# A three-pass encoder layer: later weights copied to bf16 during the first pass, conv matrices built there, and the third pass laid over buffers that the mixer frees first

## The chip, the cores and the metric

The kernel runs on all 8 cores of one Trainium2 chip, as two dies of four cores (0 to 3 and 4 to 7). The metric is device microseconds (us) of the slowest core. All cores run the same program on different rows; nothing is exchanged.

A program on all cores has a second, slower state in some executions: the cores of one die, or of both, then show a lower granted clock and the time is some per cent longer (in the first comparison one run of each kernel, 3149 and 3136 us). All comparisons below are between fast runs, or between cores of a die that kept its clock.

## The reference, cut to what matters

```python
def encoder_layer(x, ...):
    x = x + 0.5 * swiglu_ffn(x, g_ff1, w_ff1_in, w_ff1_out)      # first pass,  "A"
    z = rms_norm(x, g_mix) @ w_in                                # mixer, "B":
    cv, cg, q, k, v = jnp.split(z, SPLITS, axis=-1)
    u = cv * jax.nn.sigmoid(cg)                                  #   gated unit ...
    c_out = conv_tail(...)        # causal depthwise conv of 31 taps, layer norm, silu
    a_out = banded_window_attention(...)                         #   and attention
    x = x + jnp.concatenate([c_out, a_out], axis=-1) @ w_out     #   output projection
    x = x + 0.5 * swiglu_ffn(x, g_ff2, w_ff2_in, w_ff2_out)      # third pass, "C"
    return x, ...

def swiglu_ffn(x, g, w_up, w_down):
    a, b = jnp.split(rms_norm(x, g) @ w_up, 2, axis=-1)
    return (jax.nn.silu(a) * b) @ w_down
```

The model width is 1024 and the inner width of the feed-forward part 2816, that is 22 column groups of 128. Each core has 4096 prompt rows, 128 halo rows and 64 sample rows. Inputs and weights are fp32; the kernel multiplies in bf16.

## The kernel before

The kernel goes through its rows three times. Each pass has its own weights in SBUF, and a pass fills nearly all of SBUF, so a later pass's weights can be loaded only when an earlier pass lets go of the bytes.

Operations are recorded in program order and then put in order by a small list scheduler of the kernel's own. On each engine it may take an operation from among the first `WINDOW` that are still to be done. The order is fixed at build time, and waits come from the data that operations share.

```python
WINDOW = {"sync": 24, "scalar": 24, "vector": 24, "gpsimd": 24, "tensor": 24}
# ... Prog.schedule():
        def pick(e):
            q, h = queue[e], head[e]
            # ...
            while h < len(q) and seen < WINDOW[e]:
                u = q[h]
                h += 1
                if done[u]:
                    continue
                seen += 1
                # ... the first that is ready, or the one ready soonest
```

The feed-forward pass (used as A and as C) keeps all its weights in two tiles. The weights are fp32 in DRAM, and the loads cast them to bf16. The Trainium skill, "DMA: Bandwidth & Descriptors", section "SWDGE vs HWDGE vs iDMA", says that a cast during a DMA has to be issued from GpSimd; these loads are all on that queue.

```python
class FF:
    def __init__(self, K, off, tag, wu, wd, ...):
        C = Carve(K.P, off, tag)                       # hands out SBUF bytes in order
        self.WU = C([128, NJ, 2048], BF16, "wu")       # NJ = 22 column groups
        self.WD = C([128, NJ, 1024], BF16, "wd")
        # ... H, XNT, XA, XR, XB, XO, SA, G1, G2, SM
        self.PU = [K.pb[0], K.pb[1], K.pb[2], K.pb[3]] # PSUM banks of the up products
        self.PD = [K.pb[4], K.pb[5]]                   # and of the down products

    def load_w(self, j):
        self.O.dma("gpsimd", self.tag + "wu%d" % (j % 8), self.WU[:, j, :], self.wu[j])

    def up(self, bi, bg):                              # one block of up to 3 (first: 4) row groups
        for j in range(NJ):
            # ... 2 x 8 matmuls of 384 columns into two banks, Silu on ACT, product on DVE
            bg(1)                                      # a piece of the next block's norm
    # down(): for each row group and each half, 22 matmuls of 512 columns
```

The mixer's conv is done by matmuls against banded matrices (`wdc` in DRAM, read back as `B_wr`). They are built on DVE at the very start, between the weight loads:

```python
def conv_weights(K, off):
    # ... WB: two buffers
    def step(g):
        w = WB[g % 2]
        O.tt(w[:, :, :], EY[...], CO[:, g, :]..., ALU.mult)
        O.dma("gpsimd", "wdc%d" % (g % 2), d.wdc[g], w..., wk=[("wdc", g)])

    def prologue():
        step = conv_weights(K, A.wd_off + 15 * 2048)
        for j in range(NJ):
            A.load_w(j)
        for g in range(16):
            step(g)
        for j in range(NJ):
            A.load_d(j)
```

In the mixer the tiles matter that live to its end: `B_wo` (output weights), `B_ma` and `B_mc` (attention and conv output, transposed), `B_mt` (conv output on its way back through DRAM, `zd`), `B_wr`, `B_y`, and the three residual buffers `B_x`. The third pass was laid from the same base upward over all of this:

```python
    M = Mixer(K, base)
    M.setup()
    M.run()
    Cc = FF(K, base, "C", d.wu2, d.wd2, d.gains[2], None, ...)
    Cc.run(loads(Cc))
```

## Time and profile before

| | before |
|---|---|
| time, three runs | 2821.67, 2824.42 and (slow) 3149.47 us |
| span in the profile, slowest core (1) | 2817.9 us |
| TensorE busy | 2492 us, 88% |
| first pass, from the first down product on | 921 us |
| from the last conv product to the first down product of C | 244 us |

A row group is 128 rows, and a "down product" is one with `A_wd` or `C_wd`. Nearly every instruction goes through one helper line (L343), so the trace is read by tile names.

First, the page of the kernel before. Its 40 slices stand for 70 us each, and a digit is the share in tenths: TensorE busy, TensorE clock granted, DMA busy.

```profile
PE   1699999999999998888688962469999999999998
...
PEclk9899999999999998899799986779999999999999
DMA  9931222112221163223244559862111221111110
```

Counted from 1, TensorE is full except at the very start, in the mixer (slices 16 to 24) and in a hole in slices 25 to 27 (the digits 2, 4, 6). There DMA is the busy part, and the clock falls to 0.6.

The table of stretches of the kernel before, core 1. After each stretch come its length and then the busy time of five engines with the number of their instructions, the granted clock, the DMA share, and GB/s.

```profile
core 1: us, PE busy (x) PEld busy (x) DVE busy (x) ACT busy (x) POOL busy (x), PEclk, DMA share, GB/s
178.00:1092.00 914.00, 913.37 (x5439) 512.49 (x5439) 352.08 (x1072) 229.56 (x400) 54.72 (x81) 1.00 0.24 70
1612.10:1667.40 55.30, 39.26 (x252) 25.17 (x249) 31.07 (x63) 26.66 (x44) 10.17 (x17) 0.88 0.68 210
1667.40:1828.10 160.70, 65.81 (x262) 26.95 (x261) 44.28 (x81) 16.20 (x21) 39.55 (x72) 0.71 0.82 193
1828.10:1911.00 82.90, 55.81 (x411) 39.24 (x410) 35.42 (x127) 25.25 (x45) 9.02 (x17) 0.81 0.60 133
1715.00:1760.00 45.00, 1.01 (x2) 0.21 (x2) 0.76 (x2) 0.00 (x0) 14.83 (x27) 0.50 1.02 192
1550.00:1600.00 50.00, 48.07 (x318) 24.75 (x316) 27.02 (x60) 23.28 (x42) 7.46 (x13) 1.00 0.54 165
```

- The first pass (178 to 1092) cannot be had cheaper by moving work: 913 of 914 us busy, and DMA is only a quarter used. There is room for other DMA here.

- The casting loads reach 192 GB/s with DMA share 1.02. In another stretch 165 GB/s take a share of 0.54, which would be about 305 GB/s at full share (an estimate from that line). So bytes that a cast moves take about 1.6 times the DMA time.
- From 1715 to 1760 TensorE did 1 us of work, and its clock stands at 0.50. The Trainium skill, "TensorE: Matmul & The Clock Gate", Part 1, says that an idle window of about 3.4 us takes the clock to half. This trace agrees on the half; the 3.4 us it does not show. So idle time there costs twice: the work after it starts at half speed (four products of 1.86 us against 1.03, in the timeline below).

The chain of waits of the kernel before, core 1 (start, length, what was waited for or done):

```profile
35.53 24.49 DMA wdc<-W_wb
...
62.26 41.01 DMA wdc<-W_wb
...
173.07 5.70 DMA A_wd<-wd
...
1720.37 13.73 DMA C_wu<-wu
...
1736.39 25.41 DMA B_mt_161<-zd
...
1768.94 26.77 DMA x<-B_x_128
```

The conv matrices wait for their own stores (24 and 41 us), which stand in the GpSimd queue behind weight loads. The first down products then wait for their weights. Later, the weight loads of C make the conv output's way back (`B_mt`, 25 us) and a residual store (27 us) slow.

The timeline of TensorE in the kernel before (start, length, instruction, output<-inputs, count, and in brackets the idle time before it with what ended that):

```profile
62.10 20.52 PE L343 MATMUL PS<-A_xnt,A_wu 128*128 128x448 bf16 x96 [0.94 <-ACT A_xnt L343]
109.19 1.01 PE L343 MATMUL PS<-K_t,A_xb 128*128 128x128 bf16 x8 [26.58 <-DVE A_sm L343]
...
178.91 17.09 PE L343 MATMUL PS<-A_wd,A_h 128*128 128x512 bf16 x70 [0.63 <-DMA A_wd<-wd]
...
1740.54 1.01 PE L343 MATMUL PS<-B_wo,B_mc_145 128*128 128x512 bf16 x2 [30.14 <-DVE B_mc_145 L343]
1762.46 1.01 PE L343 MATMUL PS<-B_wo,B_mc_145 128*128 128x512 bf16 x2 [20.91 <-DVE B_mc_145 L343]
...
1804.11 1.86 PE L343 MATMUL PS<-B_wo,B_mc_145 128*128 128x512 bf16 x4 [26.16 <-DVE B_x_128 L343]
```

The hole at 82.6 in the first up run is 26.6 us. In the hand-over to C there are waits of 30.1, 20.9 and 26.2 us. Four products with `B_wo` take 1.86 us after a wait of 26 us; in an unbroken run they take 1.03.

How four late reads into `B_mt` (the four into its second buffer, tile `B_mt_161`) fared while C's weights were loaded, kernel before:

```profile
DMA to landing us min/median/max: 14.0/19.9/26.0
```

### The profile page before, as it was taken

To read this page: it belongs to the slowest core of one execution; us is meant where nothing else is said; L and a number is where in the kernel's file an instruction comes from. 1 tells how busy PE (TensorE), PEld (TensorE's weight loads), DVE (VectorE), ACT (ScalarE), POOL (GpSimd) and SP (SyncE) were. 2 spreads that over 40 slices of the span, in tenths; PEclk is the share of its full clock that TensorE was granted. 3 is DMA by queue.
4 is the path that set the end of the run, shared out by engine and by line. 5 is a ranking of instruction groups with operands and counts; after the bars stand their busy time and mean duration, and the time that the engine had idled before them with its cause. 6 is when DMAs were issued, how large, how long until landed. Compare 5 with 4: busy or idle time off the path is not lost.

```text
span 2817.9 us, 41303 instructions; the slowest of 8 cores (2803.6 to 2817.9 us)
## 1 busy us (share of the span) xinstructions
PE 2492.3 (88%) x14740; PEld 1365.4 (48%) x14740; DVE 1032.1 (37%) x2701; ACT 747.9 (27%) x1303; POOL 216.3 (8%) x380
## 2 busy tenths in 40 slices
PE   1699999999999998888688962469999999999998
PEld 0345555555555554334344530145555555555554
DVE  2243443334433333544647562143223332233211
ACT  1112222222222222545546440031112211122110
POOL 2110000000000011000111123110000000000000
PEclk9899999999999998899799986779999999999999
DMA  9931222112221163223244559862111221111110
GB/s 199 165 94 55 76 79 64 47 48 79 87 64 42 38 159 74 55 57 105 68 132 115 184 169 217 197 145 64 45 53 38 68 68 52 53 40 52 46 45 23
DMA packets 111521, 244.00 MB, mean 87 GB/s; under 512 B 32415, under 2 KB 49695, under 8 KB 111319
## 3 DMA queue, kind: packets, MB, share of 16 engines
q0 software_dynamic: 42592, 131.65, 18.4%
q1 hardware_dynamic: 68727, 109.70, 13.5%
q8 instruction: 121, 1.98, 0.3%
q14 instruction: 81, 0.66, 0.1%
HBM read 207.82 MB, written 74.79 MB: 100 GB/s over the span
## 4 chain that ended last, share of the span: by engine, by line
PE 81%; DMA 9%; DVE 4%; issue 3%; ACT 2%; POOL 0%; SPq 0%; DVEq 0%; POOLq 0%; ACTq 0%
PE PS L343 81%; DMA wdc<-W_wb 3%; DMA x<-B_x_128 1%; DMA W_ey<-eye 1%; DMA B_mt_161<-zd 1%; DMA B_mt_160<-zd 1%; DVE B_y L343 1%; DMA C_wu<-wu 0%; ACT B_pt L343 0%; DMA B_x_128<-x 0%; DMA C_xa<-x 0%; DVE W_wb L343 0%; DMA B_hc<-sconv 0%; DVE B_qn L343 0%; ACT B_sq L343 0%
## 5 line engine op out<-in xcount | busy, mean ns | idle before, releaser
L343 PE MATMUL PS<-A_xnt,A_wu 128*128 128x384 bf16 (+1 forms) x3872 | 652.8, 330 | 0.9 <-ACT A_xnt L343 0.9
L343 PE MATMUL PS<-C_xnt,C_wu 128*128 128x384 bf16 (+1 forms) x3872 | 628.5, 324 | 0.8 <-ACT C_xnt L343 0.8
L343 PEld LDWEIGHTS PS<-A_xnt,A_wu 128*128 128x128 bf16 x3872 | 378.0, 98 | 258.1 <-issue 6.4
L343 PEld LDWEIGHTS PS<-C_xnt,C_wu 128*128 128x128 bf16 x3872 | 378.2, 98 | 240.5 <-issue 1.4
L343 PE MATMUL PS<-A_wd,A_h 128*128 128x512 bf16 (+1 forms) x1496 | 329.3, 381 | 5.0 <-DMA A_wd<-wd 5.0
L343 PE MATMUL PS<-C_wd,C_h 128*128 128x512 bf16 (+1 forms) x1452 | 315.3, 379 | 0.0
L343 ACT ACTIVATE C_sa<-PS 128x384 f32<-128x384 f32 (+1 forms) x242 | 117.5, 485 | 706.3 <-PE PS L343 696.0
L343 DVE TENSOR_TENSOR C_h<-PS,C_sa 128x384 bf16<-128x384 f32 (+1 forms) x242 | 133.3, 551 | 345.9 <-PE PS L343 345.1
L343 DVE TENSOR_TENSOR A_h<-PS,A_sa 128x384 bf16<-128x384 f32 (+1 forms) x242 | 136.0, 563 | 308.4 <-PE PS L343 307.6
L343 ACT ACTIVATE A_sa<-PS 128x384 f32<-128x384 f32 (+1 forms) x242 | 119.7, 495 | 430.2 <-PE PS L343 379.9
L343 PEld LDWEIGHTS PS<-A_wd,A_h 128*128 128x128 bf16 (+1 forms) x1496 | 146.7, 98 | 179.4 <-issue 9.1
L343 PEld LDWEIGHTS PS<-C_wd,C_h 128*128 128x128 bf16 (+1 forms) x1452 | 142.4, 98 | 169.9 <-issue 0.4
L343 DVE SCALAR_TENSOR_TENSOR C_xr<-PS,C_xr 128x512 f32<-128x512 f32 (+1 forms) x66 | 45.6, 691 | 281.3 <-PE PS L343 281.3
L343 PE MATMUL PS<-B_xn,B_wi 128*128 128x512 bf16 x512 | 126.5, 398 | 8.5 <-DVE B_t_76 L343 3.4
L343 PE MATMUL PS<-K_t,A_xb 128*128 128x128 bf16 (+1 forms) x544 | 42.9, 224 | 84.1 <-DVE A_sm L343 62.6
L343 PE MATMUL PS<-B_us,B_wr 128*128 128x256 bf16 (+1 forms) x576 | 88.2, 309 | 30.2 <-DVE B_qkt L343 17.6
L343 DVE SCALAR_TENSOR_TENSOR A_xr<-PS,A_xr 128x512 f32<-128x512 f32 (+1 forms) x68 | 46.9, 690 | 163.3 <-PE PS L343 163.1
L343 PE MATMUL PS<-B_wi,B_xn 128*128 128x256 bf16 (+1 forms) x512 | 92.6, 335 | 8.3 <-ACT B_pt L343 8.3
L343 PE MATMUL PS<-B_wo,B_mc_145 128*128 128x512 bf16 x64 | 20.7, 453 | 83.0 <-DVE B_mc_145 L343 51.0
L343 ACT ACTIVATE A_xb<-A_xr 128x1024 bf16<-128x1024 f32 (+1 forms) x34 | 35.8, 1053 | 201.5 <-DVE A_xr L343 201.5
L387 POOL DMA_DIRECT2D yout<-C_xr x33 | 17.6, 535 | 928.2 <-DVE C_xr L343 928.2
L343 ACT ACTIVATE B_pt<-PS 128x1024 bf16<-128x1024 f32 (+1 forms) x68 | 66.1, 984 | 78.6 <-PE PS L343 78.6
(167 smaller groups left out, 2029.4 us busy)
## 6 DMA issues: line engine op xcount, KB each, us to landing
B_wr<-wdc SPq DMA_DIRECT2D x32, 576.0 KB, 5.0
A_xa<-xin SPq DMA_DIRECT2D x33, 512.0 KB, 3.9
A_xr<-xin SPq DMA_DIRECT2D x33, 512.0 KB, 3.6
x<-A_xr POOLq DMA_DIRECT2D x33, 512.0 KB, 3.0
C_xr<-x SPq DMA_DIRECT2D x32, 512.0 KB, 3.7
C_xa<-x SPq DMA_DIRECT2D x32, 512.0 KB, 3.7
yout<-C_xr POOLq DMA_DIRECT2D x32, 512.0 KB, 2.9
A_wu<-wu POOLq DMA_DIRECT2D x22, 512.0 KB, 37.1
```

The costliest lines, as they stand in the source:

```text
L343: o = self.P.add(eng, lambda e: getattr(e, meth)(**kw), r, w, cost=self.cost(eng, meth, kw))
L387: self.P.add(eng, lambda e: e.dma_start(out=out, in_=in_), r, w, lane=lane, rk=rk, wk=wk, cost=1.0 if eng == "gpsimd" else 0.5, nbytes=n * ...
```

## The change

The intent has three parts.

1. Start: no conv matrices between the first pass's weights. They are built in 32 halves during the first pass, in buffers of that pass (`XO`).
2. Copies: all later weights (`w_in`, `w_out`, and the third pass's two) are cast once, DRAM to DRAM, in 60 casting copies spread over the first pass. Later loads then are plain bf16 copies from the sync queue and carry half the bytes from DRAM.
3. Layout: C's tiles are put where the mixer frees its bytes first. The first 11 up weights lie over projection and attention tiles, the other 11 over the conv tiles. C has other PSUM banks for its up products. The scheduling window goes from 24 to 64, so that C's first norms and up products can be placed among the last output projections.

The diff, cut to its core:

```diff
-WINDOW = {"sync": 24, "scalar": 24, "vector": 24, "gpsimd": 24, "tensor": 24}
+WINDOW = {"sync": 64, "scalar": 64, "vector": 64, "gpsimd": 64, "tensor": 64}
...
+        fits = NJ if low is None else (low - c1.off) // 4096
+        self.WU = [(c1 if j < fits else c2)([128, 2048], BF16, "wu") for j in range(NJ)]
...
-        self.PU = [K.pb[0], K.pb[1], K.pb[2], K.pb[3]]
-        self.PD = [K.pb[4], K.pb[5]]
+        self.PU = [K.pb[2], K.pb[4], K.pb[3], K.pb[5]]
+        self.PD = [K.pb[0], K.pb[1]]
...
     def load_w(self, j):
-        self.O.dma("gpsimd", self.tag + "wu%d" % (j % 8), self.WU[:, j, :], self.wu[j])
+        k = [("pc", self.tag + "u", j)] if self.weng == "sync" else []
+        self.O.dma(self.weng, self.tag + "wu%d" % (j % 8), self.WU[j][:, :], self.wu[j], rk=k)
...
+    def hook(bi, j):
+        if bi == 0:
+            return
+        if j % 3 == 1 and casts:
+            t, k, dst, src = casts.pop(0)
+            O.dma("gpsimd", "pc%d" % (k % 4), dst, src, wk=[("pc", t, k)], after=P.last["vector"])
+        if j % 5 == 3 and convs:
+            wstep[0](*convs.pop(0))
...
     def prologue():
-        step = conv_weights(K, A.wd_off + 15 * 2048)
-        for j in range(NJ):
-            A.load_w(j)
-        for g in range(16):
-            step(g)
-        for j in range(NJ):
-            A.load_d(j)
+        loads(A)()
+        wstep[0] = conv_weights(K, cr, lambda: A.XO[A.nxt("xo", 2)])
...
-    Cc = FF(K, base, "C", d.wu2, d.wd2, d.gains[2], None, ...)
+    c0 = Carve(P, base, "C")
+    c2 = Carve(P, M.US_off, "C_")
+    Cc = FF(K, (c0, c0, c2), "C", d.wu2b, d.wd2b, d.gains[2], None, ..., low=M.mid, weng="sync")
```

## The prediction

> **What bounds the kernel now.** By the table of stretches: three PE-bound passes with two DMA holes. First pass, 178 to 1092 us: PE 913 of 914 us busy, clock 1.00, DMA share 0.24. Mixer, 1092 to 1710: PE 503 of 618, limited by short ACT/DVE/PE dependencies. Third pass, 1883 to 2817: PE 99% busy, clock 1.00. The holes:
> - Start (chain of waits, 0 to 179 us): the conv matrices' DVE products wait for their own stores (24.5 and 41.0 us), which queue behind weight casts; norms and gating sit behind them on DVE. PE idles 26.6 us at 82.6; down starts at 169, stalls, and runs freely from 178.9.
> - Mixer to third pass, 1710 to 1883: PE busy 63 of 173 us at clock 0.66, DMA share 0.88 at 188 GB/s. Casting weight loads start at 1715; the B_mt reads then take 20-25 us instead of 4, residual traffic waits likewise (chain: 25.4, 26.8, 13.7 us).
>
> **What DMA costs.** Casting loads move 196 GB/s (of destination) at share 1.0; elsewhere 165 GB/s take only 0.54, about 305 GB/s per full share. So 17.3 MB of third-pass weights cost about 88 us as casts, about 57 us as bf16 copies (estimates from those figures). The Trainium skill, "DMA: Bandwidth & Descriptors", section "Issuing engines are not separate DMA queues", says queues share the same 16 engines; the trace agrees: a sync-queue A_xa load took about 31 us under casts, median 3.9.
>
> **What the change does.**
> 1. Start: no conv matrices between weights. The third row block's x still lands near 50 us, so up products start near 60 as now, then run without the hole: 352 matmuls at about 0.19 us = 67-70 us; down starts near 132-135, weights landed (about 21 MB/196 = 107 us). Gain: about 40 us.
> 2. Sixty casts (23 MB, about 120 us of DMA) and 32 DVE products of about 0.7 us spread over the first pass: DMA share about 0.4, PE above 98%. Loss 0 to 10 us.
> 3. Mixer: work unchanged; the wider scheduling window leaves PE order nearly the same. Within 15 us either way.
> 4. Third pass: 11 of 22 up weights overlay attention buffers, so they load during the conv tail (DMA share 0.6 there; may cost the tail 10 us); first norms and half of the first up run among the last out-projections, on other PSUM banks. Only 11.5 MB remain. Of the 173-us hole about 52 us is PE work at full clock; I expect 10-25 us of stalls left (last up and down weights, after the last out-projection). Gain 90-105 us.
>
> Sum: 40 + 97 + 5 - 5 = about 140 us, nearly all on the critical path. Predicted 2680 us, range 2635 to 2730. Faster by over 2%: 0.95; within 2%: 0.04; slower: 0.01.
>
> **What would show it.** Step 1: first long down run starts at 130-140, PE dense from about 60. Step 2: PE 98% or more at clock 1.00 in the first pass. Step 4: weight issues from the sync queue start when attention ends; B_mt reads land in under 8 us; PE holes between mixer and third pass total under 40 us. Mixer length (first pass end to last conv matmul, now about 580 us) within 15 us.
>
> **What would make it wrong.** First-pass residual traffic caught behind casts, or ACT's copies waiting for the buffers that conv stores share, would stall PE there. Early weight loads on the in-order sync queue could hold up conv-matrix and history loads, lengthening the tail by tens of us. The order is static: a wait the scheduler misjudged now blocks more. Conversely, if the mixer packs better, the time falls below 2650.

## More of the kernel before

- Between the last conv product (1667) and the first down product of C (1911) TensorE is busy for 66 and then 56 us, 122 of 244. The other 122 us are idle.

## The result, and the profile after

| | before | after |
|---|---|---|
| median of four runs each | 2823.14 us | 2731.5 us |
| fast runs | 2821.67, 2821.85, 2824.42 | 2720.68, 2724.05, 2738.95 |
| slow run | 3149.47 | 3135.9 |
| ratio of fast runs, 95% | | 0.9664 [0.9608, 0.972] |
| span in the profile, slowest core | 2817.9 (core 1) | 2722.3 (core 3) |
| TensorE busy | 88% | 92% |

A ratio is the mean time of one kernel's fast runs over that of the other's of the same rounds, so it is not quite the ratio of the medians. The medians here also carry the one slow run of each kernel.

The change took about 95 us here, and 102 us in a later measurement (run after_again below, 0.9636). The prediction was a gain of about 140. The direction and most of the size came; some 40 us did not.

To see where, each profile was cut into stages by the starts of the first and last matmuls of a group. The figures are means over cores 0 to 3 in us, from starts read to whole us, so a stage is good to about half a us and a sum to about one:

| stage (from, to) | before | after | difference |
|---|---|---|---|
| start: 0 to the first down product of A | 166.8 | 125.3 | -41.5 |
| A: to the last down product of A | 920.8 | 927.8 | +7.0 |
| attention: to the last product of `B_pt` (p times v) | 519.0 | 522.3 | +3.3 |
| conv tail: to the last conv product | 55.0 | 69.3 | +14.3 |
| outputs: to the last output projection | 159.5 | 132.0 | -27.5 |
| C: to the last down product of C | 979.8 | 930.3 | -49.5 |
| sum | 2800.8 | 2706.8 | -94.0 |

The page of the kernel after, read as before:

```profile
PE   2999999999999998887779965789999999999998
...
PEclk9999999999999999898979988899999999999999
DMA  9943353334442253122234584661111122111110
```

TensorE is full from slice 2, and slices 25 to 27 have 5, 7, 8 where 2, 4, 6 stood (a slice is now 68 us). DMA is a little busier through the first pass, as intended.

The table of stretches of the kernel after, on its slowest core 3:

```profile
133.00:1054.00 921.00, 919.39 (x5482) 515.50 (x5483) 374.20 (x1114) 229.86 (x401) 96.28 (x160) 1.00 0.39 102
1581.00:1647.00 66.00, 40.68 (x243) 25.53 (x242) 30.80 (x62) 28.34 (x48) 7.51 (x13) 0.84 0.74 245
1647.00:1783.00 136.00, 94.02 (x505) 48.67 (x503) 78.91 (x224) 36.65 (x55) 28.11 (x49) 0.87 0.61 194
1783.00:1824.00 41.00, 35.52 (x245) 23.79 (x244) 6.35 (x13) 8.03 (x16) 0.53 (x1) 0.92 0.76 248
```

The first pass keeps 919 of 921 us busy at clock 1.00 with DMA share 0.39. From the last conv product (1647) to C's first down product (1824) there are 177 us in place of 244, and TensorE is busy for 94 + 35.5. Idle are 42 + 5.5 = 47.5 us in place of 122. The conv tail before it grew to 66 us here.

The chain of waits of the kernel after, core 3:

```profile
133.03 234.38 PE PS L347 x1395
...
1582.41 23.31 DMA B_wr<-wdc
...
1624.83 7.64 DMA B_wr<-wdc
...
1687.63 9.64 DMA B_x_152<-x
...
1782.49 6.57 DMA C_wu<-wu2b
```

The conv products now wait for their matrices (`B_wr`, 23.3 and 7.6 us in the chain), which they scarcely did before. The 25 us waits for `B_mt` and the residual store are gone. What remains of their kind is a residual load of 9.6 us and one of C's late up weights (6.6 us).

The timeline of TensorE of the kernel after, core 3:

```profile
54.24 60.30 PE L347 MATMUL PS<-A_xnt,A_wu 128*128 128x448 bf16 x304 [0.94 <-ACT A_xnt L347]
...
133.03 5.12 PE L347 MATMUL PS<-A_wd,A_h 128*128 128x512 bf16 x23 [0.89 <-DMA A_wd<-wd]
...
1605.85 3.63 PE L347 MATMUL PS<-B_us,B_wr 128*128 128x256 bf16 x18 [6.84 <-DMA B_wr<-wdc]
...
1707.73 10.53 PE L347 MATMUL PS<-C_xnt,C_wu 128*128 128x320 bf16 x64 [0.84 <-ACT C_xnt L347]
...
1789.20 33.86 PE L347 MATMUL PS<-C_xnt,C_wu 128*128 128x320 bf16 x224 [5.48 <-DMA C_wu<-wu2b]
```

Up products start at 54, run without the hole, and the first pass is in a free run of down products at 133 instead of 179. C's first up products stand at 1708, in the middle of the output projections. The rest wait for a weight at 1789.

The waits of TensorE in the kernel after, core 3, from 1581 to 1854 (who waited for what; total us, times, longest us):

```profile
PE PS L347 <- DVE B_mc L347: 13.0, 2, 7.2
PE PS L347 <- DVE C_xb L347: 12.7, 4, 5.0
...
PE PS L347 <- DVE B_x_152 L347: 9.8, 3, 6.2
...
PE PS L347 <- DMA C_wu<-wu2b: 5.5, 1, 5.5
...
PE PS L347 <- DVE B_x_153 L347: 3.6, 1, 3.6
```

No single wait of the size of before (30, 26 and 21 us) is left; what is left is many short ones.

The four late reads into the second `B_mt` buffer (here tile `B_mt_180`), the kernel after, as shown for before:

```profile
DMA to landing us min/median/max: 4.6/6.4/8.0
```

### The profile page after: what moved, and what is told of

The parts are those of the page before. It is cut to its first block, busy times and chain, and to the rows that moved or that the text cites. A ratio compares the mean times of both kernels' runs of the same rounds, so it can differ in the third digit from the quotient of the medians.

```text
span 2722.3 us, 41562 instructions; the slowest of 8 cores (2711.5 to 2722.3 us)
## 1 busy us (share of the span) xinstructions
PE 2494.1 (92%) x14740; PEld 1364.6 (50%) x14740; DVE 1032.7 (38%) x2717; ACT 750.5 (28%) x1303; POOL 223.3 (8%) x398
## 4 chain that ended last, share of the span: by engine, by line
PE 81%; DMA 9%; DVE 4%; issue 3%; ACT 2%; POOL 0%; DVEq 0%; POOLq 0%; ACTq 0%; SPq 0%
PE PS L347 81%; DMA A_wd<-wd 4%; DMA B_wr<-wdc 1%; DMA C_wu<-wu2b 1%; DMA B_x_152<-x 1%; DMA B_mt_179<-zd 1%; DVE B_y L347 1%; DMA B_xn<-xnt 0%; DVE C_sm L347 0%; DMA A_wu<-wu 0%; ACT B_pt L347 0%; DVE B_qn L347 0%; ACT B_sq L347 0%; DVE B_z L347 0%; DMA B_x_153<-x 0%
## 5 line engine op out<-in xcount | busy, mean ns | idle before, releaser
L347 PE MATMUL PS<-B_us,B_wr 128*128 128x256 bf16 (+1 forms) x576 | 91.9, 319 | 24.7 <-DMA B_wr<-wdc 11.2
L391 POOL DMA_DIRECT2D yout<-C_xr x33 | 17.6, 534 | 912.2 <-DVE C_xr L347 903.1
L347 PEld LDWEIGHTS PS<-B_us,B_wr 128*128 128x128 bf16 x576 | 61.1, 110 | 53.4 <-issue 34.4
L347 PEld LDWEIGHTS PS<-B_xn,B_wi 128*128 128x128 bf16 x512 | 49.3, 102 | 72.2 <-issue 26.5
```

What stands on the lines that cost most here:

```text
L347: o = self.P.add(eng, lambda e: getattr(e, meth)(**kw), r, w, cost=self.cost(eng, meth, kw))
L391: self.P.add(eng, lambda e: e.dma_start(out=out, in_=in_), r, w, lane=lane, rk=rk, wk=wk, cost=1.0 if eng == "gpsimd" else 0.5, nbytes=n * ...
```

## The experiments

Twelve kernels were run, all with correct results. They were made in three groups of four, each group on one chip with the kernel before beside it. The stage table is again the mean over cores 0 to 3 of the profiled run, in us, with the sum last. (In the profile of slots one die was slow; cores 0 to 3 were not.)

| run | start | A | attention | tail | outputs | C | sum |
|---|---|---|---|---|---|---|---|
| before | 166.8 | 920.8 | 519.0 | 55.0 | 159.5 | 979.8 | 2800.8 |
| start_only | 129.0 | 920.3 | 521.8 | 54.8 | 162.3 | 980.5 | 2768.5 |
| win64_only | 166.3 | 926.3 | 531.5 | 105.3 | 115.8 | 984.3 | 2829.3 |
| third_casts | 124.8 | 927.8 | 520.8 | 78.8 | 139.8 | 943.3 | 2735.0 |
| after_win24 | 129.0 | 923.0 | 514.3 | 68.5 | 112.3 | 974.5 | 2721.5 |
| after | 125.3 | 927.8 | 522.3 | 69.3 | 132.0 | 930.3 | 2706.8 |
| after_again | 124.8 | 927.3 | 522.3 | 68.5 | 130.5 | 931.3 | 2704.5 |
| old_banks | 124.5 | 929.5 | 521.5 | 70.5 | 124.3 | 944.5 | 2714.8 |
| conv_store_sync | 124.8 | 926.8 | 522.3 | 70.0 | 130.5 | 930.5 | 2704.8 |
| weights_actq | 125.0 | 928.5 | 522.8 | 61.3 | 133.8 | 930.0 | 2701.3 |
| hold_weights | 124.8 | 928.3 | 523.8 | 55.8 | 131.5 | 931.0 | 2695.0 |
| slots | 124.3 | 929.3 | 521.8 | 68.5 | 131.8 | 922.3 | 2697.8 |
| slots_hold | 125.3 | 925.3 | 520.3 | 56.5 | 131.8 | 922.8 | 2681.8 |
| slots_hold_mix | 128.5 | 921.3 | 513.8 | 57.5 | 132.8 | 924.3 | 2678.0 |

The two profiles of the same changed kernel (after and after_again, measured apart) agree within 1.5 us in every stage, and in the sum within 2.3 us.

### One part of the change at a time

These four were run together. The kernel before had fast runs of 2829.7 us in the mean on this chip.

**start_only**: the kernel before with the new start alone. The conv matrices are built in the first pass as in the changed kernel; there are no copies, and the layout and window are those of before.

```diff
     def prologue():
-        step = conv_weights(K, A.wd_off + 15 * 2048)
-        ... (weights and conv steps in turn)
+        loads(A)()
+        wstep[0] = conv_weights(K, CE, lambda: A.XO[A.nxt("xo", 2)])
...
+    def hook(bi, j):
+        if bi and j % 5 == 3 and convs:
+            wstep[0](*convs.pop(0))
```

> The kernel before with the start of the change alone: first-pass weights loaded without conv matrices between them, the 32 conv products and stores spread over the first pass, no casts, window 24, third pass as before. Main theory: the start and the third pass's entry are independent, so this takes the whole 46 us off the start (down runs freely from about 133 instead of 179 us), and without casts ahead of them on the queue the conv stores cost the first pass 0 to 3 us: 2775 to 2785 us, 40 to 46 us under before. Rival: the 8 us that the first pass lost in the changed kernel come from the sharing of the transpose buffers alone, with or without casts: then 36 to 39 us under before, and PE shows the same three stalls in the first pass.

Measured: fast runs 2786.2 to 2802.9, mean 2794.3, ratio 0.9878 [0.9837, 0.9918], so 35 us. By stages the first pass ends 38 us earlier (1087.5 to 1049.3) and 32 us arrive at the end. The start of the change is worth its predicted 40 us within a few us, and it needs nothing else. My own figure of 40 to 46 us was missed all the same: the gain at the end of the first pass is 38, and attention and outputs give 3 us each back, for which I have no cause. The 32 conv products and their stores cost the first pass nothing: on core 1 the blocks of up and down products follow each other every 88.4 us, as before, so the stalls that the rival asked for are not there.

**win64_only**: the kernel before with the wide scheduling window alone.

```diff
-WINDOW = {"sync": 24, "scalar": 24, "vector": 24, "gpsimd": 24, "tensor": 24}
+WINDOW = {"sync": 64, "scalar": 64, "vector": 64, "gpsimd": 64, "tensor": 64}
```

> The kernel before with the scheduling window 64 instead of 24 and nothing else. Main theory: the order of PE in the mixer hardly changes and the third pass's buffers lie over ones that are freed late, so within 8 us of before (2815 to 2830). Rival: the wider window is what lets the third pass start early; then 20 us or more under before (2800 or less).

Measured: fast runs 2843.9 to 2859.2, mean 2850.5, ratio 1.0076 [1.0031, 1.0121]. It is 21 us slower, and neither theory had that. The table of stretches of this run, core 1, its conv tail:

```profile
1625.70:1729.70 104.00, 43.35 (x253) 26.23 (x249) 30.44 (x61) 26.40 (x44) 15.67 (x29) 0.72 0.96 209
```

The conv tail took 104 us instead of 55, at DMA share 0.96, with TensorE only 43 us busy. The first pass, too, ended about 5 us later (stage A +5.5). The window moves instructions on every queue, not on TensorE alone: the first casting load of C was issued at 1621 instead of 1715, into the tail, and the conv matrices' reads then landed after up to 24.7 us on the slowest core (9.7 before). They are on the sync queue and the casting loads on the GpSimd queue, so standing in one line is not needed for a slow landing. Attention is 12 us longer too, ahead of all those loads, and I have no wait that explains it; the reordering itself is the only difference there.

**third_casts**: the changed kernel, but the third pass's weights are again cast as they are loaded (from the GpSimd queue), with no copies of them in the first pass. Layout and window stay.

```diff
-    for j in range(NJ):
-        casts += [("Cu", j, d.wu2b[j], d.wu2[j]), ("Cd", j, d.wd2b[j], d.wd2[j])]
...
-    Cc = FF(K, (c0, c0, c2), "C", d.wu2b, d.wd2b, ..., low=M.mid, weng="sync")
+    Cc = FF(K, (c0, c0, c2), "C", d.wu2, d.wd2, ..., low=M.mid)
```

> The changed kernel, but the third pass's weights are not copied in the first pass: they are cast from f32 by gpsimd loads, in the new layout and with window 64. Main theory: casts move 196 GB/s against about 305, so 17.3 MB cost some 31 us more of DMA where DMA is scarce, and they stand on the queue of the conv-output reads and residual loads; minus up to 8 us that the first pass wins back: 15 to 45 us over the changed kernel (2740 to 2770). Rival: only the early start counts and DMA rate is not what binds; then within 8 us of the changed kernel or under it.

Measured: fast runs 2756.4 to 2773.5, mean 2764.0, ratio 0.9771 [0.9731, 0.981]; by stages 28 us over the changed kernel (30.5 over after_again), spread over tail (+9.5), outputs (+8) and C (+13). That is what the third pass's copies are worth. The table of stretches shows DMA as the limit, core 1 of this run, from the last output projection to the first down product:

```profile
1786.60:1837.90 51.30, 35.49 (x250) 24.14 (x249) 10.76 (x36) 10.72 (x20) 13.93 (x27) 0.91 1.06 195
```

DMA is full, and full means 195 GB/s while casting. The bf16 copies reach 299 GB/s at share 0.94 in the last run below. The prediction had put the third pass's 17.3 MB at 88 us as casts and 57 us as copies; that difference, 31 us, is close to what came. It is not proof that the rate is the whole cause: a cast is issued from GpSimd, so this edit also moves the loads from the sync queue to the GpSimd queue, where the residual rows and the conv output go. On core 1 of this run a residual store issued at 1597 took 24 us to land (7 us for the one at 1598 in the changed kernel), and the last eight reads into `B_mt` took up to 15 us (12). No run separates the rate from the queue.

**after_win24**: the changed kernel with the old window. The edit is the reverse of the line shown for win64_only.

> The changed kernel with window 24 instead of 64. Its static order still issues 11 up-weight loads during the conv tail, but the first up products come after the last out-projections instead of before them. Main theory: the 24 us of up products no longer fill the wait for the last conv matrices, part of which opens again: 10 to 25 us over the changed kernel (about 2735 to 2748). Rival 1: the window gives most of the third-pass gain, then 50 us or more over. Rival 2: the layout does it all and PE only shifts work, then within 5 us.

Measured: fast runs 2738.3 to 2738.8, mean 2738.5, ratio 0.9681 [0.9637, 0.9725]. The ratio cannot be told from that of the changed kernel. The stages can: C's first up products stand after the last output projection again, which costs outputs and C together 25 us, while attention gains 8 us and the first pass 1 us. So the wide window buys what it was for, at the hand-over, and pays a third of it back in attention, where nobody wanted it. (In this run the start looks 4 us longer and A 5 us shorter; under conv_store_sync below this turns out to be a boundary that moved.)

From start_only, third_casts and the changed kernel the parts can be read from the stage sums: 32 us for the start, 33.5 us for layout, window and the mixer's bf16 weights, and 28 us for the third pass's copies.

### What holds up the conv tail, and what the first pass pays

These four were run together on another chip; the kernel before had fast runs of 2834.6 us in the mean. All edits are made to the changed kernel.

**hold_weights**: C's up weights may be issued only after the last read of conv matrices.

```diff
+        self.weng, self.hook, self.hold = weng, hook, None
...
-        self.O.dma(self.weng, ..., self.WU[j][:, :], self.wu[j], rk=k)
+        self.O.dma(self.weng, ..., self.WU[j][:, :], self.wu[j], rk=k, after=self.hold)
...
+    Cc.hold = max(P.lane_last["bwr0"], P.lane_last["bwr1"])
     Cc.run(loads(Cc))
```

> The changed kernel, but no third-pass weight load is issued before the last conv-matrix load has landed. Main theory: the conv tail (last attention product to last conv product) took 67 us instead of 55 because the weight loads stand before the conv-matrix loads on the sync queue (one took 23 us to land, median 4.7); held back, every such load lands in under 10 us and the tail takes 53 to 58 us. The weights then fall among residual traffic, so at most part of the 11 us stays: total between 10 us under and 5 us over the changed kernel. Rival: the tail is longer through the order of DVE and ACT under the wider window; then it stays at 64 us or more with all loads quick.

Measured: fast runs 2711.2, 2711.3 and 2722.3, mean 2714.9, ratio 0.9578 [0.9535, 0.9621]. The tail is back to 56 us, and C does not get longer, so the saving stays whole: 12 us by stages. The reads of conv matrices, issue to landing, first in the changed kernel and then with the hold (each its slowest core):

```profile
L391 SPq DMA_DIRECT2D B_wr<-wdc x32: 359/376/2690, 1055.4 to 1636.5; - x32
...
DMA to landing us min/median/max: 3.7/4.7/23.3
```

```profile
L391 SPq DMA_DIRECT2D B_wr<-wdc x32: 359/376/972, 1058.5 to 1623.9; - x32
...
DMA to landing us min/median/max: 3.7/5.2/11.3
```

The longest landing falls from 23.3 to 11.3 us, and the longest issue on the queue from 2.7 us (2690 ns) to 1.0. The early weights did not need to be that early: C waits no longer for the ones that were held.

**weights_actq**: C's weights issued from the ACT queue instead of the sync queue. The aim was to issue them as early as before.

```diff
...                                            # in load_w and load_d: the waits on the copies stay
-            low=M.mid, weng="sync")
+            low=M.mid, weng="scalar")
```

> The changed kernel with the third pass's weights issued from the ACT queue instead of the sync queue, as early as before. If the conv-matrix loads wait because they stand in line behind weights on one queue, they now land in under 10 us, the tail is 55 to 60 us, and the total is 3 to 12 us under the changed kernel. If they wait because 16 shared engines are full, the longest landing stays at 15 us or more and the tail at 64 us or more, total within 5 us.

Measured: fast runs 2733 to 2741, ratio 0.9658 [0.9631, 0.9685]. In each of these runs some cores had a clock of 0.96 where the others had 0.97 (cores 4 and 5 in the profiled run), and those set the time, so only the stages of cores 0 to 3 are used. There the tail is 61 us, between 69 and 56, although the longest landing of the conv matrices is still about 20 us.

The issues of C's up weights, first in the changed kernel and then here (each its slowest core), show that the edit did more than change the queue:

```profile
L391 SPq DMA_DIRECT2D C_wu<-wu2b x22: 319/338/3590, 1557.5 to 1792.2; - x22
```

```profile
L391 ACTq DMA_DIRECT2D C_wu<-wu2b x22: 326/327/1135, 1579.3 to 1782.1; - x22
```

The first weight was issued 2 us after the last p times v product, where the changed kernel issues it 23 us before that product (the same on cores 0 to 3 of both). The two reads of conv matrices that are issued around that product landed in 6 to 9 us instead of 14 to 23, and the next two in 18 to 20 (cores 0 to 3). So the weights were not issued as early as before, and the run cannot tell the other queue from the later issue.

The Trainium skill, "DMA: Bandwidth & Descriptors", section "Issuing engines are not separate DMA queues", says that a second issuer only saves the time on the sequencer, since all share 16 engines. The slow landings agree with that, and so does win64_only above, where the weights and the reads were on two queues. The same page, "Queues, rings and completion order", says that the engines go round between the rings that have work and take each ring in order, which would let a read on another ring pass part of the weights. Whether that was so here is not shown: the 8 us that came back may be the later issue alone. Holding the weights back removes all of it.

**conv_store_sync**: the stores of the conv matrices, in the first pass, from the sync queue instead of the GpSimd queue where the casts are.

```diff
-        O.dma("gpsimd", "wdc%d" % h, d.wdc[g][:, 576 * h:576 * h + 576], w, wk=[("wdc", g, h)])
+        O.dma("sync", "wdc%d" % h, d.wdc[g][:, 576 * h:576 * h + 576], w, wk=[("wdc", g, h)])
```

> The changed kernel with the first pass's conv-matrix stores issued from the sync queue instead of behind the casts on gpsimd. Main theory: the 7 to 8 us by which the first pass's body is longer (928 against 921 us from first down product to last) are ACT and DVE waiting for transpose buffers whose stores stand behind casts (wdc<-A_xo waits of 4.4 and 2.0 us before PE stalls): body 919 to 923 us, total 5 to 9 us under the changed kernel. Rival: sharing these buffers costs it whatever the queue; then 926 to 930 us and no gain.

Measured: fast runs 2723.3 to 2739.6, ratio 0.9654 [0.9611, 0.9697]: no clear gain, 2 us by stages. My expectation rested on a misread number: I had taken the 7 us by which stage A grew for the cost of casts and stores. Timing each block from its first down product to the next, on core 1, shows otherwise:

| block interval, us | window | first | the eight after it | last |
|---|---|---|---|---|
| before | 24 | 99.8 | 88.4 each | 85.7 |
| start_only | 24 | 98.8 | 88.4 each | 85.7 |
| after_win24 | 24 | 98.8 | 88.4 to 88.9 | 86.6 |
| win64_only | 64 | 103.1 | 88.4 each | 87.4 |
| after | 64 | 102.6 | 88.4 to 88.9 | 86.6 |
| conv_store_sync | 64 | 105.0 | 88.4 to 88.8 | 86.6 |

The first interval grows with the wide window, casts or not. With the new start it grows by about as much as the start shrinks (after_win24 to after: 3.5 against 3.9 us, means of cores 0 to 3): the window sets the first down product about 4 us earlier, and the first pass ends no earlier for it (at 1052.0 in after_win24, at 1053.0 in after, means of cores 0 to 3). That was a boundary of my stages that moved, not work. (win64_only is different: there the start shrinks by less than 1 us, and the first pass really ends 5 us later.) What the copies cost can be read from start_only and after_win24, of one chip and with one window: the first pass ends at 1049.3 without the copies and at 1052.0 with them. So 60 casts of 23 MB cost it about 3 us. Core 1 alone hides part of this: over the eight blocks, cores 0 to 3 of the changed kernel lose 1.0 to 5.1 us (mean 2.5), and here 0.6 to 1.3 (mean 0.9). So some 2 us of my theory were there.

**old_banks**: the up and down products of both feed-forward passes on the PSUM banks of the kernel before.

```diff
-        self.PU = [K.pb[2], K.pb[4], K.pb[3], K.pb[5]]
-        self.PD = [K.pb[0], K.pb[1]]
+        self.PU = [K.pb[0], K.pb[1], K.pb[2], K.pb[3]]
+        self.PD = [K.pb[4], K.pb[5]]
```

> The changed kernel with the old PSUM banks: up products on banks 0 to 3, down products on 4 and 5, so the first up products share banks 0 and 1 with the last out-projections. Main theory: the up products cannot run between the two last groups of out-projections, so the wait for the last conv matrices opens again and 24 us of PE work move behind it: 10 to 25 us over the changed kernel. Rival: the scheduler fills it otherwise; within 5 us.

Measured: fast runs 2730.6 to 2733.4, ratio 0.964 [0.9621, 0.9659]. By stages it is 8 us slower: outputs -8, C +14. This lies between the two theories. With the old banks more of C is left for after the last output projection; the new ones are worth under 10 us, and the ratio does not tell the two kernels apart.

### A version that beats both

These four ran together on a third chip, in five rounds. The kernel before had fast runs of 2823.2 us in the mean.

**after_again**: the changed kernel as it is, as the measure for the other three.

> The changed kernel unaltered, as the measure for the three others on the same chip: ratio to before 0.962 to 0.970, conv tail 66 to 71 us, last conv product to last out-projection 129 to 137 us, from there to the end 929 to 932 us.

Measured: fast runs 2720.5 to 2722.9, mean 2721.7, ratio 0.9636 [0.9619, 0.9653]. The stages repeat.

**slots**: the 11 late up weights keep the same bytes as a set, but are dealt out in another order, so that the weights that are used first lie where the mixer frees its tiles first.

```diff
+        if low is not None:
+            self.WU[fits:] = [self.WU[fits + i] for i in (6, 7, 4, 5, 2, 3, 10, 8, 9, 0, 1)]
```

> The changed kernel with another assignment of up-weight tiles to the buffers that the mixer frees late: the buffer under the third conv output, free only after the last out-projection, holds the last two tiles of the pass instead of tiles 12 and 13. Theory: what is left of the hole after the last conv product is PE without ready work while the out-projections wait for the last layer norm and residual loads; ten of the other eleven tiles' products can now run there, and the 5.5 us wait for tile 12 vanishes: 8 to 18 us under the changed kernel, last out-projection to end under 915 us. Rival: shared DMA engines bind, tiles do not arrive earlier, and PE work only changes places: within 4 us.

Measured: fast runs mean 2714.4, ratio 0.961 [0.9592, 0.9629]; 7.2 us less than after_again, all of it in C (931 to 922). It is the direction of the main theory and just under its size; C did not get under 915, and the wait for a late weight did not vanish. From 1640 to 1830, in means of cores 0 to 3, TensorE waited 3.9 us for late up weights instead of 6.4, with 2.6 for down weights that are new, and 3.0 us instead of 8.6 for residual rows (`B_x`). So the other order mostly gave TensorE work to do while the residual rows came.

**slots_hold**: slots, hold_weights and conv_store_sync together.

```diff
+            self.WU[fits:] = [self.WU[fits + i] for i in (6, 7, 4, 5, 2, 3, 10, 8, 9, 0, 1)]
+    Cc.hold = max(P.lane_last["bwr0"], P.lane_last["bwr1"])   # and after=self.hold in load_w
-        O.dma("gpsimd", "wdc%d" % h, ...)
+        O.dma("sync", "wdc%d" % h, ...)
```

> The same assignment, weight loads held until the last conv-matrix load has landed, and conv stores on the sync queue. If the effects of holding (about 14 us in the profile) and of the assignment (about 12 us) add up: 20 to 30 us under the changed kernel, tail 54 to 58 us. If held loads then arrive too late for the products that should fill the hole: 8 to 16 us under it.

Measured: fast runs mean 2701.5, ratio 0.9567 [0.9549, 0.9586]; 20.1 us less than after_again and 12.9 less than slots. The tail is 56.5 and C 922.8: the effects add.

**slots_hold_mix**: as slots_hold, with the window at 24 until attention ends and 64 from there.

```diff
+        wide = ops[self.wide].unit          # first operation recorded after the last attention step
...
-            while h < len(q) and seen < WINDOW[e]:
+            limit = WINDOW[e] if h < len(q) and q[h] >= wide else 24
+            while h < len(q) and seen < limit:
```

> As slots_hold, with the scheduling window 24 until attention ends and 64 from there on. The changed kernel with window 24 throughout had an attention part about 8 us shorter (514 against 522 us over cores 0 to 3) and lost more than that at the third pass's entry; with both windows the first should be kept and the second not: 4 to 10 us under slots_hold. Rival: the 8 us came from something else than the window's reach in attention (a different landing of the conv tail): within 3 us of slots_hold.

Measured: fast runs 2690.6 to 2693.1, mean 2692.0, ratio 0.9531 [0.9512, 0.955]; 9.6 us less than slots_hold. (The slowest core makes this look large: the mean of all cores over the fast runs fell by 6.9 us, the stage sum of cores 0 to 3 in the profiles by 3.8.) Attention is 514 us, as in after_win24, and the hand-over keeps its overlap. This is the best kernel: 131 us under the kernel before and 30 us under the change as it was made. Its table of stretches, core 1, the outputs and then the rest to the first down product of C:

```profile
1622.30:1754.30 132.00, 109.29 (x630) 60.34 (x628) 76.78 (x205) 38.17 (x60) 23.96 (x42) 0.90 0.70 226
1754.30:1782.70 28.40, 18.21 (x123) 11.70 (x121) 11.44 (x47) 9.08 (x15) 0.53 (x1) 0.81 0.94 299
```

In the outputs TensorE is now busy for 109 of 132 us (in the changed kernel 94 of 136 on core 3). In the last 28 us DMA is nearly full, with plain copies at 299 GB/s: here DMA looks like the limit of the hand-over, which no further run tested.

## Why the prediction was right or wrong

The predicted time was 2680 us in a range of 2635 to 2730, and faster by over 2% at 0.95. The ratio 0.9664 is faster by over 2%. The median of 2731.5 lies 1.5 us above the range, with one slow run in it; the fast runs lie on both sides of its upper edge, and those of after_again within it. So the class was right, and the centre was 40 to 50 us too low. By steps:

1. **Start: "Gain: about 40 us".** Right. Up products run without the hole from 54 to 126, and the free run of down products begins at 133 ("132-135"). start_only shows that this part alone ends the first pass 38 us earlier. Only the first up product came at 54, not "near 60". (The 41.5 us of the stage table hold about 4 that the window only moved to the next stage.)

2. **Copies in the first pass: "Loss 0 to 10 us", "DMA share about 0.4, PE above 98%".** Right: share 0.39, clock 1.00, 919 of 921 us busy, about 3 us lost. Start and A together gained 34.5 us, against 38.3 in start_only.

3. **Mixer: "the wider scheduling window leaves PE order nearly the same. Within 15 us either way".** From the end of the first pass to the last conv product the length grew by 14 us on core 1 (577 to 591) and by 17.6 in the mean of cores 0 to 3, so at the edge of that. The sum had counted the mixer as 5 us gained. This is the first term that failed. The tail, 14 of these us, is the next point; in attention alone 3.3 us were lost where 5 were counted as gained. What I missed is that a window acts in the mixer too. win64_only shows that it moves the issue of DMAs (the first weight load of C from 1715 to 1621) and costs 21 us by itself. And with the window narrow until attention ends the attention stage is 6.5 us shorter (slots_hold to slots_hold_mix); by what way the window lengthens it is not shown.

4. **The conv tail: "may cost the tail 10 us".** It cost 14, and the text named the cause: early weights that hold up the conv matrices. hold_weights takes the 14 us back, so that much is shown. That it is the order in the sync queue, and not the shared DMA engines, is not. And the 10 us were not in the sum.

5. **Hand-over: "I expect 10-25 us of stalls left ... Gain 90-105 us".** The mechanism was right: of the 77 us that outputs and C gained, third_casts gives 21 to the copies and after_win24 about 25 to C's early up products; the other 30 or so fall to the layout by subtraction, which was not run alone. The size was off. Outputs and C together gained 77 us, not 97, because 47.5 us of TensorE idle time are left between the last conv product and C's first down product ("under 40" was the mark). The term that was mis-sized is this one, the stalls. By the waits of core 3 shown above, they are made of 13.0 us for `B_mc`, 12.7 for norms (`C_xb`), 13.4 for residual rows (the two `B_x` lines) and 5.5 for a late weight. The prediction allowed for the weights alone, after the last output projection. There it had 10 to 25 us, and only 5.5 came; the other 42 us lie among the output projections, where the sum had named none. About 7 of the 20 us were the order of the late weights in memory (slots); the rest is spread over those short waits.

Added up, in the stages: 34.5 for the first pass (predicted 40 less 5), -3.3 for attention (predicted +5 for the mixer), -14.3 for the tail (not in the sum) and 77.0 for the hand-over (predicted 97) make the 94 measured, against 137 predicted. Three small repairs gave back 30 us in measured time.

**The marks in the profile.** `B_mt` was to land in under 8 us: the four reads shown took 4.6 to 8.0, at the edge, against 14 to 26 before, but two late reads into the other buffer took 11.5 and 12.6 (core 3), so this mark was missed. The weights' issue was to begin when attention ends: it began at 1557.5, some 23 us before the last p times v product.

**What stays open.** Why attention gets 6 to 12 us longer under the wide window was not traced to a wait; only that it does, in three pairs of kernels. Nor was it separated whether the conv matrices waited for the order in their queue or for the shared engines, or what of the copies' gain is rate and what is queue. And no repair was aimed at the waits for residual rows (13.4 us in the changed kernel), though slots shortened them: a fourth residual buffer takes 4096 bytes per partition, and the mixer's layout ends at byte 229056 of 229344.

## What to carry to other kernels

Work that a full engine hides is nearly free: 60 casting copies in a pass at DMA share 0.24 cost about 3 us, and the 44 of them for the third pass took 28 to 31 us out of a place where DMA was the limit. When later loads are made possible earlier, ask what they will overtake: issuing them as early as the memory allows cost the reads that came after them 14 us of the conv tail, and an order ("after the last read of the current stage") gave that back without loss. And a scheduling knob turned for one place acts everywhere and on every queue, so confine it to the place it is meant for, and let the stalls that remain be a term of the sum, one for each kind of wait seen in the old profile.

## What the Trainium skill lacked or had wrong

- "DMA: Bandwidth & Descriptors" (sections "SWDGE vs HWDGE vs iDMA" and "Rules for kernel authors") says where a cast has to be issued but gives no rate for it. Here casting loads took the whole DMA share for 195 GB/s of destination, bf16 copies moved 299 GB/s at share 0.94. An estimate from such figures put that difference at 31 us for the third pass's weights, and 28 to 31 us came, queue and rate together.
- The same page, "Issuing engines are not separate DMA queues", says that spreading issues over engines only saves sequencer time. No run here speaks against that. What it leaves out is that the other issuer also sets when the loads start: on the ACT queue C's weights were first issued 25 us later, against the end of attention, than on the sync queue, and the conv tail was 8 us shorter.
- "TensorE: Matmul & The Clock Gate", Part 1, tells the reader, for the default power profile, to budget 13/16 of the clock for sustained dense matmul on all cores. In the fast runs here all eight cores worked together and the first pass shows a clock of 1.00 over 914 us. A block of 352 products of 384 columns and 132 of 512 took 88.4 us, 2.29 columns per ns, which 1.95 GHz could not give. In the slow run of the changed kernel one die stood at 0.81 to 0.82 in the mean and the other at 0.97. The page does not say that the limiter may stay away for a whole run.
- No page gives a figure for a read that is issued behind other loads on its queue. Here the longest landing of the conv matrices' reads went from 9.7 us to 23.3 when C's weights were issued ahead of them, and to 11.3 when these were held back.
